# Where the softmax denominators of a streaming encoder layer are added up: diagonal exponentials on GpSimd and VectorE, one ones-product a step

## The chip, the cores and the metric

The kernel runs on one core of a Trainium2 chip. Its time is the device time of one execution in microseconds; the time of a kernel is the median of its runs. The engines that matter are TensorE (PE, with its weight loads listed apart as PEld), VectorE (DVE), ScalarE (ACT), GpSimd (POOL) and the queues that issue DMAs (SP's above all).

## What is computed

One layer of a hybrid encoder, in one step for 2048 new frames of a prompt and for 8 streams of 16 frames each that have 1024 cached frames. The part that the change touches is the attention of both groups, with 8 heads of 64 columns:

```python
def _attend(q, k, v, cum_q, cum_k, q_pos, k_pos):
    s = jnp.einsum('bqhd,bkhd->bhqk', q, k, preferred_element_type=jnp.float32) * (HEAD_DIM ** -0.5)
    s = s + (cum_q[..., :, None] - cum_k[..., None, :])
    mask = k_pos[None, :] <= q_pos[:, None]
    s = jnp.where(mask, s, NEG_INF)
    p = jax.nn.softmax(s, axis=-1)
    return jnp.einsum('bhqk,bkhd->bqhd', p.astype(v.dtype), v)
```

Before it lie the conditioning, a normalisation and the input projection, beside it a convolution branch with a normalisation over channels, and behind it the output projection and a gated feed-forward network. All of it is in 32-bit floats.

## The kernel before

The kernel goes through the stages in order: input projections, queries and keys, attention (627 to 1187 us of the span), output projection, feed-forward network.

**Steps of the attention.** The prompt's attention is 16 steps: four pairs of heads `p` by four blocks of 512 queries `qb`. A step goes over `4 * qb + 4` tiles of 128 keys (`kt`). For each tile and each of the two heads `h`, TensorE makes the scores `s` with keys on the partitions and queries on the columns (lines 1035 and 1041, with a mask product on line 1043 where the tile lies on the diagonal), and ScalarE makes the exponentials `e` (line 1045). The last four tiles of a step are the diagonal ones; their columns begin at `off` = 0, 128, 256 and 384, so they are 512, 384, 256 and 128 wide. Two tiles later `values` adds the product of `e` with V into the bank `pv` (line 999).

**Denominators.** The sum of the exponentials over the keys is a sum over partitions, done with a product by a matrix of ones 32 columns wide into the bank `sm` (`add_up`, line 988). Each of the four groups of 32 PE columns holds a term. For tiles before the diagonal the exponentials are first added up elementwise into two tiles `sums`: those of head 0 by GpSimd (line 1011), those of head 1 by VectorE (line 1012, shown under the helper's line 1105). Diagonal tiles went to TensorE one by one: at the second diagonal tile four products of 512 columns (the two `sums` and the first diagonal tile; in the steps with `qb` = 0, which have no tile before the diagonal, the first two diagonal tiles), and at the fourth the rest. `end_of_step` copies `sm`, sends its rows to memory, brings them back turned, inverts them on VectorE and multiplies `zc` by the inverse; the last step does it with a product by `four` on TensorE instead, into a bank of the group `cv`.

**Maxima.** The exponentials need the largest score of each query. A second pass of score products (`mx`, line 952, with a mask product on line 956 at the diagonal) runs ahead of the scores, and VectorE reduces each to its maximum (`M`, line 957). There are 320 of them, two PSUM banks (`cv`), and they run up to `LEAD` = 48 tiles ahead in the order of emission.

**Order.** A scheduler orders each engine's instructions by priority, with extra order edges written by hand (`after`). Three matter here. A score product may not stand before the `last_product` emitted ahead of it, so ones-products hold the scores back (line 1038). A score product stands behind a maximum's product 32 to 42 tiles ahead. And every VectorE operation issued through `late(..., self.last_max)` stands behind the last maximum emitted by then. Each engine works through its list in order.

**Background.** Into the steps are woven the channel normalisation of the convolution branch (`conv_norm`, tiles `cy`, `cm`, `cr`, `cq`; its GpSimd operations stand behind the last addition of exponentials) and the attention of the eight streams (`sample_scores`, `sample_values`; tiles `S`, `ST`, `En`, `rsx`, `lane`). A stream's denominators were eight products with one column: for each of four pairs of heads one of `rsx` (sums over cached keys) with `fold`, and one of `EnT` (the new frames) with ones.

## Time and profile before

| | us |
|---|---|
| median of 3 runs | 2798.58 |
| the three runs | 2797.13, 2798.58, 2804.48 |
| profiled execution | 2804.35 |
| its span | 2802.6 |
| attention in the span | 627 to 1187 |

The profiled execution was 5.77 us above the median. Columns of the rows below: a group's row gives line, engine, operation, output and inputs, then count, busy microseconds and the mean of one in nanoseconds, then the idle time before them and what ended it. A row in order of time gives start and length in microseconds. A 32-bit product of TensorE shows as two records, a score product as one.

### The profile page before, as it was taken

What the parts mean: (1) busy time and instruction counts of PE and PEld (TensorE: products, weight loads), DVE (VectorE), ACT (ScalarE), POOL (GpSimd) and SP (SyncE); (2) the same over time, 40 slices, a digit from 0 to 9 for tenths busy, and PEclk for the clock granted to TensorE, in tenths of its full rate; (3) what the DMA queues carried; (4) which work ended last, traced back from release to release, by engine and by line L of the source; (5) the groups of instructions that cost most, each with busy time, mean ns of one, the idle gap of its engine ahead of it and who ended that gap; (6) DMA issues with size and microseconds to landing.
All of it is one profiled execution on the core that took longest, in us unless ns stands there. A gap on an engine that the chain in (4) does not pass through costs nothing. (4 is left out here: it accounts for less than half of the span.)

```text
span 2802.6 us, 49271 instructions
## 1 busy us (share of the span) xinstructions
PE 2734.4 (98%) x17042; PEld 2407.4 (86%) x17042; DVE 2023.4 (72%) x4116; ACT 1235.4 (44%) x2472; POOL 499.6 (18%) x678
## 2 busy tenths in 40 slices
PE   7999999999999999999999999999999999999999
PEld 6999988864445555499999999999999999999999
DVE  2798898964656666545397989877887778676765
ACT  4543323343444333444354446444554446555552
POOL 3555411323443121214201121000000000000000
PEclk9999999989999999999999999999999999999999
DMA  9753568673536576165576869866786769787873
GB/s 330 252 186 115 186 213 269 200 201 87 149 94 199 163 238 211 53 219 185 168 262 209 300 198 313 282 213 214 248 279 213 224 194 319 243 288 254 277 250 116
DMA packets 416978, 603.57 MB, mean 215 GB/s; under 512 B 65140, under 2 KB 280340, under 8 KB 414680
## 3 DMA queue, kind: packets, MB, share of 16 engines
q1 hardware_dynamic: 416520, 600.05, 67.1%
q8 instruction: 134, 2.20, 0.3%
q14 instruction: 116, 0.95, 0.1%
q0 software_dynamic: 208, 0.37, 0.0%
HBM read 426.00 MB, written 174.25 MB: 214 GB/s over the span
## 5 line engine op out<-in xcount | busy, mean ns | idle before, releaser
L1663 PE MATMUL z<-rT,rW 128*128 128x360 f32 (+1 forms) x8316 | 1382.8, 328 | 4.6 <-ACT eU L1682 1.2
L1663 PEld LDWEIGHTS z<-rT,rW 128*128 128x128 f32 x8316 | 1378.6, 188 | 6.8 <-DVE e L1685 1.8
L1367 ACT ACTIVATE rW<-rR 128x512 fp32r<-128x512 f32 x714 | 434.8, 617 | 391.1 <-PE z L1663 274.4
L1368 DVE TENSOR_TENSOR rW<-rR,rW 128x512 fp32r<-128x512 f32 x714 | 477.8, 674 | 162.6 <-ACT rW L1367 159.1
L712 DVE SCALAR_TENSOR_TENSOR cv<-cu,cpar,cv 128x384 f32<-128x384 f32 x580 | 311.6, 614 | 2.3 <-ACT cv L710 2.2
L957 DVE TENSOR_REDUCE M<-mx 128x1 f32<-128x512 f32 (+2 forms) x320 | 190.6, 605 | 167.8 <-PE mx L952 125.0
L1045 ACT ACTIVATE e<-s 128x512 f32<-128x512 f32 (+3 forms) x320 | 166.4, 531 | 291.6 <-PE s L1041 165.0
L524 PE MATMUL z<-hqx,wqh 128*128 128x384 f32 (+1 forms) x768 | 197.6, 333 | 1.4 <-DVE logf L359 1.4
L1367 ACT ACTIVATE rT<-traw 128x360 fp32r<-128x360 f32 (+1 forms) x315 | 149.6, 501 | 86.8 <-DMA traw<-gt_d 53.8
L1368 DVE TENSOR_TENSOR rT<-traw,rT 128x360 fp32r<-128x360 f32 (+1 forms) x315 | 157.9, 531 | 38.0 <-ACT rT L1367 37.5
L999 PE MATMUL pv<-e,V 128*64 128x512 f32 (+3 forms) x640 | 158.7, 569 | 0.0
L952 PE MATMUL mx<-K,Q 96*128 96x512 f32 (+2 forms) x320 | 142.8, 460 | 11.8 <-DVE M L957 10.7
L952 PEld LDWEIGHTS mx<-K,Q 96*128 96x128 f32 x320 | 62.6, 198 | 103.7 <-DVE M L957 48.1
L524 PEld LDWEIGHTS z<-hqx,wqh 128*128 128x128 f32 x768 | 136.1, 188 | 17.8 <-issue 12.4
L1351 PE MATMUL acc<-ch,woh 128*128 128x360 f32 (+1 forms) x384 | 128.2, 336 | 8.5 <-ACT ch L1367 3.4
L1035 PE MATMUL s<-Q,K 128*128 128x512 f32 (+3 forms) x320 | 131.5, 411 | 0.0
L1351 PE MATMUL acc<-ch,wol 128*128 128x360 f32 (+1 forms) x384 | 128.1, 334 | 0.0
L524 PE MATMUL z<-hqx,wql 128*128 128x384 f32 (+1 forms) x384 | 126.6, 330 | 0.0
L1591 DVE TENSOR_TENSOR rR<-rR 128x512 f32<-128x512 f32 (+1 forms) x136 | 93.2, 703 | 44.7 <-DMA rR<-w_down 41.8
L1351 PE MATMUL acc<-cl,woh 128*128 128x360 f32 (+1 forms) x384 | 123.9, 333 | 0.0
L1041 PE MATMUL s<-Q,K 128*128 128x512 f32 (+3 forms) x320 | 120.2, 375 | 0.0
L1011 POOL TENSOR_TENSOR sums<-e,sums 128x512 f32<-128x512 f32 x72 | 93.9, 1304 | 115.9 <-ACT e L1045 114.9
(316 smaller groups left out, 3746.8 us busy)
## 6 DMA issues: line engine op xcount, KB each, us to landing
rR<-sup_d SPq DMA_DIRECT2D x176, 256.0 KB
rR<-w_gate SPq DMA_DIRECT2D x132, 256.0 KB
traw<-gt_d SPq DMA_DIRECT2D x154, 180.0 KB
rR<-w_down SPq DMA_DIRECT2D x104, 256.0 KB
rR<-sdn_d SPq DMA_DIRECT2D x96, 256.0 KB
rR<-w_up SPq DMA_DIRECT2D x88, 256.0 KB
sup_d<-rR SPq DMA_DIRECT2D x88, 256.0 KB
wa<-w_ada SPq DMA_DIRECT2D x16, 1024.0 KB
```

The lines of the kernel that those rows point to most:

```text
L524: nc.tensor.matmul(z[:, :n], w[:, m], x[:, :n], start=(c == 0 and k == 0), stop=(c == CB - 1 and k == 2))
L712: self.pin(nc.vector.scalar_tensor_tensor(dst, src, w, acc[i], ALU.mult, ALU.add))
L952: self.mx.append(nc.tensor.matmul(mx[:, :w], Q2[0:AUX, h, j * P:(j + 1) * P], K2[kb][0:AUX, h, :w], start=True, stop=not diag))
L957: self.last_max = nc.vector.tensor_reduce(M[:, i, kb:kb + 1], mx[:, :w], AX.X, ALU.max)
L999: product = nc.tensor.matmul(z[0][HD * h:HD * h + HD, off:], V[kt // 4][:, kt % 4, HD * h:HD * h + HD], es[h][:, off:], start=(kt == 0), s ...
L1035: first = nc.tensor.matmul(s[:, off:], K1[kb][:, h, sl], Q1[:, h, off:], start=True, stop=False)
L1041: self.last_s = nc.tensor.matmul(s[:, off:], K2[kb][:, h, sl], Q2[:, h, off:], start=False, stop=not diag)
L1045: self.last_piece = nc.scalar.activation(e[:, off:], s[:, off:], AF.Exp)
L1351: self.nc.tensor.matmul(z[:, :n], w[:, m], y, start=(first and i == 0 and k == 0), stop=(last and i == len(terms) - 1 and k == 2))
L1367: copy = self.nc.scalar.activation(hi, raw, AF.Copy)
L1368: engine.tensor_tensor(lo, raw, f32(hi), ALU.subtract)
L1663: nc.tensor.matmul(z, W[:, x, m], t[:, y, :w], start=(k == 0 and i == 0), stop=(k == n - 1 and i == 2))
```

## The change

1. Exponentials of all tiles, the diagonal ones too, are added into the two `sums` tiles, by GpSimd for head 0 and VectorE for head 1 (`settle`). It is called before the second score of the tile after, and not two tiles later with the values. In the steps with `qb` = 0 the first 128 columns are copied first.
2. A step makes its two ones-products once, over 512 columns, after its last value product.
3. `sm` has 64 rows and two parts instead of four, so fewer DMAs, and VectorE's addition of the two parts goes.
4. The last step's spread goes into the bank `ss` (the lane's) instead of one of `cv`.
5. A stream's denominators: VectorE adds the new frames' sums to `rsx`, GpSimd multiplies them into `parts` (128x128), and TensorE makes one product with ones.
6. `conv_norm` yields once more before its second mean.

```diff
-        def add_up(terms, last=False):
-            if not started:
-                z.append(self.bank("tr", "sm"))
+        def add_up(out, terms):
             behind = self.last_product
-            for i, (g, o, x) in enumerate(terms):
-                self.last_product = nc.tensor.matmul(z[1][32 * g:32 * g + 32, o:], self.ones[:, 0:32], x[:, o:], start=(g not in started),
-                                                     stop=last and g not in [t[0] for t in terms[i + 1:]], tile_position=(0, 32 * g))
+            for h, x in enumerate(terms):
+                self.last_product = nc.tensor.matmul(out[32 * h:32 * h + 32], self.ones[:, 0:32], x, start=True, stop=True, tile_position=(0, 32 * h))
                 self.after(self.last_product, behind)
+
+        def settle(kt, off, es):
+            dve = lambda op, *args: self.late(op, self.last_max)(*args)
+            if kt == 0:
+                held.extend(es)
+                return
+            x, y = held
+            if kt == 1:
+                acc.extend(wk.tile([P, 512], F32, tag="acc", name="sums", bufs=4) for h in range(2))
+                if off:
+                    nc.gpsimd.tensor_copy(acc[0][:, :off], x[:, :off])
+                    dve(nc.vector.tensor_copy, acc[1][:, :off], y[:, :off])
+            else:
+                x, y = acc
+            self.last_add = nc.gpsimd.tensor_tensor(acc[0][:, off:], es[0][:, off:], x[:, off:], ALU.add)
+            dve(nc.vector.tensor_tensor, acc[1][:, off:], es[1][:, off:], y[:, off:], ALU.add)
...
-            if d == 3:
+            if kt == nkt - 1:
                 zc = wk.tile([P, 512], F32, tag="zc", name="zc")
                 self.last_exp = nc.scalar.copy(zc, z[0])
-                add_up(held, True)
-                self.end_of_step(p, qb, zc, z[1])
-            elif d == 1:
-                n = 4 if qb else 2
-                add_up(held[:n])
-                del held[:n]
+                sums = self.bank("tr", "sm")
+                add_up(sums, acc)
+                self.end_of_step(p, qb, zc, sums)
...
             for h in range(2):
+                if h and self.unsettled:
+                    self.unsettled.pop(0)()
...
                 if h:
+                    self.unsettled.append(partial(settle, kt, off, es))
                     self.waiting.append((values, kt, off, es))
...
-            spread = self.bank("cv", "R")
-            nc.tensor.matmul(spread, self.four, sm, start=True, stop=True)
+            spread = self.bank("ss", "R")
+            nc.tensor.matmul(spread, self.two, sm, start=True, stop=True)
...
-            if qb:
-                self.after(nc.vector.tensor_tensor(w[:, 0], w[:, 0], w[:, 1], ALU.add), self.last_max)
-            self.after(nc.vector.reciprocal(w[:, 0], w[:, 0]), self.last_max)
+            self.after(nc.vector.reciprocal(w, w), self.last_max)
...
+        rn = sm.tile([32, NP], F32, tag="rn", name="rn")
+        parts = sm.tile([P, NP, 32], F32, tag="parts", name="parts")
+        self.dve("tensor_reduce", rn, self.En[:, :, :QS], AX.X, ALU.add)
+        self.dve("tensor_tensor", rs[:32], rs[:32], rn, ALU.add)
+        self.gp(parts, self.fold.unsqueeze(1).broadcast_to([P, NP, 32]), rs.unsqueeze(2).broadcast_to([P, NP, 32]), ALU.mult)
...
-        for g in range(NP):
-            r = slice(32 * g, 32 * g + 32)
-            self.pe(den[r], self.fold, rs[:, g:g + 1], start=True, stop=False, tile_position=(0, 32 * g))
-            self.pe(den[r], EnT[:QS, g], self.ones[:QS, 0:1], start=False, stop=True, tile_position=(0, 32 * g))
+        self.pe(den, parts.rearrange("p g r -> p (g r)"), self.ones[:, 0:1], start=True, stop=True)
```

What this does to the order is seen at three places. The first is TensorE's list at the end of the third step (`p` = 0, `qb` = 2). Before, from the first ones-product (the numbers behind names are buffers; `masks` products belong to the maximum ahead of them):

```order
L988 MATMUL sm_7897<-sums_7610,ones_115 32x512 [waits Pool_49]
L952 MATMUL mx_7804<-K25_6650,Q21_6636 128x128 [waits DVE_49]
L956 MATMUL mx_7804<-masks_4135 128x128
L952 MATMUL mx_7818<-K24_6647,Q21_6636 128x512 [waits DVE_49]
L952 MATMUL mx_7831<-K25_6650,Q21_6636 128x256 [waits DVE_49]
L956 MATMUL mx_7831<-masks_4135 128x128
L968 MATMUL pz_7835<-ident_99,Z_0_6621 128x128 [waits DVE_49]
L988 MATMUL sm_7897<-sums_7611,ones_115 32x512 [waits DVE_49]
L988 MATMUL sm_7897<-e_7777,ones_115 32x512
L988 MATMUL sm_7897<-e_7798,ones_115 32x512
```

The same place after the change:

```order
L988 MATMUL sm_7952<-sums_7578,ones_115 32x512 [waits Pool_49]
L954 MATMUL mx_7881<-K24_6647,Q21_6636 128x512 [waits DVE_49]
L954 MATMUL mx_7904<-K25_6650,Q21_6636 128x512 [waits DVE_49]
L958 MATMUL mx_7904<-masks_4135 128x128
L954 MATMUL mx_7913<-K24_6647,Q21_6636 128x512 [waits DVE_49]
L954 MATMUL mx_7925<-K25_6650,Q21_6636 128x128 [waits DVE_49]
L958 MATMUL mx_7925<-masks_4135 128x128
L954 MATMUL mx_7940<-K24_6647,Q21_6636 128x512 [waits DVE_49]
L988 MATMUL sm_7952<-sums_7579,ones_115 32x512 [waits DVE_49]
L1034 MATMUL s_7965<-Q1_7644,K10_6633 128x512 [waits Activation_49]
```

Between the ones-product of GpSimd's sums and that of VectorE's stood three maxima products, and now five. Before, ten of the sixteen steps had two to nine maxima there, 35 in all (the four steps with `qb` = 0 had no such place, and the last two steps none left); now fourteen steps have them, 80 in all: thirteen in the first step, seven in the second, five in each of the twelve after. The last two steps have none, and their two ones-products stand side by side.

The second place is VectorE's list there, after the change:

```order
L959 TENSOR_REDUCE M_1_6656<-mx_7881 128x1
L1103 TENSOR_TENSOR sums_7579<-e_7865,sums_7579 128x256
L1095 TENSOR_TENSOR zc_7551<-zc_7551,aR_7558 128x512
L959 TENSOR_REDUCE M_1_6656<-mx_7904 128x1
L959 TENSOR_REDUCE M_1_6656<-mx_7913 128x1
L1103 TENSOR_TENSOR sums_7579<-e_7898,sums_7579 128x128
L959 TENSOR_REDUCE M_1_6656<-mx_7925 128x1
L959 TENSOR_REDUCE M_1_6656<-mx_7940 128x1
```

The last addition (128 columns, buffer `e_7898`), for which the second ones-product waits, moved behind the third of the five maxima; the last diagonal tiles had no addition on VectorE before.

The third place is GpSimd's list at the end of the eighth step (`p` = 1, `qb` = 3), where the last chunk of `conv_norm` ends. Before:

```order
L1105 TENSOR_TENSOR cy<-cy,cmu 128x128 x4
L1011 TENSOR_TENSOR sums<-e,sums 128x512 x4
L1105 TENSOR_TENSOR cy<-cy,cr 128x128 x4
L1153 MEMSET En 32x128
L1156 MEMSET Qbd 128x1024
```

After:

```order
L1103 TENSOR_TENSOR cy<-cy,cmu 128x128 x4
L1005 TENSOR_TENSOR sums<-e,sums 128x512 x5
L1005 TENSOR_TENSOR sums<-e,sums 128x384
L1005 TENSOR_TENSOR sums<-e,sums 128x256
L1103 TENSOR_TENSOR cy<-cy,cr 128x128 x4
L1005 TENSOR_TENSOR sums<-e,sums 128x128
```

The step's last addition, which the first ones-product waits for, now stands behind the four operations on `cr`; before, no ones-product had to wait for anything behind them in this step.

## The prediction

> **What bounds the kernel now.** The page comes first: TensorE is busy nearly all the time, so only what TensorE does or waits for can move the end. Then the table by windows, for the attention alone (columns after the length: busy microseconds and count of PE, PEld, DVE, ACT, POOL, then the granted TensorE clock, the DMA share and GB/s).

> ```profile
> PE 2734.4 (98%) x17042; PEld 2407.4 (86%) x17042; DVE 2023.4 (72%) x4116; ACT 1235.4 (44%) x2472; POOL 499.6 (18%) x678
> 627.00:1187.00 560.00, 547.29 (x3607) 283.68 (x3606) 326.54 (x678) 227.74 (x513) 165.88 (x164) 0.98 0.51 150
> ```

> Of 560 us TensorE shows 12.7 idle; VectorE is 58% busy, GpSimd 30%. The view of waits says who waits for whom in the same stretch:

> ```profile
> ACT e L1045 <- PE s L1041: 165.0, 115, 11.4
> PEld mx L952 <- DVE M L957: 40.0, 59, 3.1
> ```

> ScalarE's exponentials wait for TensorE, not the reverse. The one engine that TensorE often waits for is VectorE, in the maxima pass with its two banks. So the attention is bound by TensorE, with VectorE close behind where maxima stand thick.

> **Part 1, the ones-products.** The first row counts the records of line 988 in the attention. I price each product by its slot, the time from its start to the start of what follows it, in the list of TensorE's instructions in order of time:

> ```profile
> 627.00:1187.00 560.00, 51.48 (x304) 11.86 (x304) 0.98 0.51 150
> ...
> 1046.70 1.05 PE L988 MATMUL sm<-sums,ones 128*32 128x512 f32 x2
> 1047.68 0.33 PE L1105 MATMUL lane<-ident,ob 128*128 128x128 f32 x1
> ...
> 1050.80 0.62 PE L988 MATMUL sm<-e,ones 128*32 128x512 f32 x2
> ...
> 1051.78 0.50 PE L1035 MATMUL s<-Q,K 128*128 128x512 f32 x1
> ...
> 1056.11 1.27 PE L988 MATMUL sm<-e,ones 128*32 128x384 f32 x12
> 1057.31 0.39 PE L1035 MATMUL s<-Q,K 128*128 128x256 f32 x1
> 637.40 1.49 PE L988 MATMUL sm<-e,ones 128*32 128x384 f32 x12
> 638.82 0.50 PE L952 MATMUL mx<-K,Q 96*128 96x512 f32 x1
> ```

> A single product of 512 columns has a slot of 0.98 us; three side by side in other column groups (1050.80) have 0.98 too. The six smaller ones have 1.20, or 1.42 where `qb` = 0. Before, then: twelve steps of 0.98 + 0.98 + 1.20 = 3.16, which is 37.9, and four of 0.98 + 1.42 = 2.40, which is 9.6; 47.5 in all. After, by the order shown above, fourteen steps issue their two products apart (1.96) and two issue them together (0.98): 29.4. **Gain 18.1 us**, on the path, since nothing covers TensorE.

> **Part 2, the wait between the two.** The scores of the next tiles are held until the second product is issued, and TensorE has only maxima (and lane work) to do until VectorE's last addition is through. The trace has this place already, shorter:

> ```profile
> 887.62 0.73 PE L952 MATMUL mx<-K,Q 96*128 96x512 f32 x2
> 888.90 0.44 PE L952 MATMUL mx<-K,Q 96*128 96x384 f32 x1 [0.56 <-DVE M L957]
> ...
> 889.63 0.62 PE L988 MATMUL sm<-e,ones 128*32 128x512 f32 x2
> 886.02 0.42 DVE L957 TENSOR_REDUCE M<-mx 128x1 f32<-128x256 f32 x1
> 888.16 0.69 DVE L957 TENSOR_REDUCE M<-mx 128x1 f32<-128x512 f32 x1 [1.72 <-PE mx L952]
> 888.88 0.69 DVE L1105 TENSOR_TENSOR sums<-e,sums 128x512 f32<-128x512 f32 x1
> L957 DVE TENSOR_REDUCE M<-mx 128x1 f32<-128x512 f32 (+2 forms) x283 | 170.0, 608 | 162.5 <-PE mx L952 122.1 <-PE mx L956 39.1
> ```

> It lasts from 887.62 to 889.63, 2.01 us: 0.54 until the first maximum starts on VectorE, one maximum, one addition. TensorE's own work in it is three maxima at about 0.37 (0.73 for the first two), 1.1, so 0.9 is lost. After, three maxima and the additions of 256 and 128 columns stand before the second product: 0.54 + 3 x 0.69 + 0.42 + 0.24 = 3.27. The two additions have no row; I take the 0.42 of a maximum 256 wide, and 0.24 as an estimate for half of that. TensorE's work is 5 x 0.37 = 1.85, so 1.42 is lost, 0.52 more than before. Nine steps of 0.52 are 4.7. Three steps with `qb` = 0, which had no such place, lose 1.42 each, 4.3. The first step gets thirteen maxima, eleven before its last addition: 0.54 + 11 x 0.69 + 1.4 for four operations is 9.5, less 4.8 of work, so 4.7. The second step had nine maxima and now has seven:

> ```profile
> 655.90 0.73 PE L952 MATMUL mx<-K,Q 96*128 96x512 f32 x2
> ...
> 662.79 1.06 PE L988 MATMUL sm<-sums,ones 128*32 128x512 f32 x1
> ```

> From 6.9 less 3.3 of work to about 5.2 less 2.6: a gain of 1.0. **Loss 12.7 us.** Bounds: nothing, if the rounds behind a burst, which then have fewer maxima, run as much faster; and 45 more maxima at 0.608, 27 us, if none of their TensorE work is saved elsewhere. I keep 12.7, the count from the rows.

> **Part 3, more additions.** A step had `4 * qb - 1` additions on each engine where `qb` is above 0, and now has `4 * qb + 3`: 144 instead of 84, and four copies.

> ```profile
> L1105 DVE TENSOR_TENSOR sums<-e,sums 128x512 f32<-128x512 f32 x72 | 58.3, 809 | 1.8 <-ACT e L1045 1.3
> L1011 POOL TENSOR_TENSOR sums<-e,sums 128x512 f32<-128x512 f32 x72 | 93.9, 1304 | 115.9 <-ACT e L1045 114.9
> ```

> On GpSimd they cost at most 60 x 1.3 = 78 us, to 244 of 560, hidden as long as its list isn't blocked (first rival). On VectorE some 30 have their price in part 2. The other 32 stand among maxima in ordinary rounds and delay a bank's return. Bounds: nothing, or 0.81 each, 26 us. I take TensorE's idle time of before over the additions of before, 12.7 / 84 = 0.15: **loss 4.8 us**.

> **Part 4, a stream's denominators.**

> ```profile
> 1038.69 0.22 PE L1105 MATMUL lane<-rsx,fold 128*32 128x1 f32 x2
> ...
> 1039.89 0.64 PE L1105 MATMUL lane<-kc,Qbd 128*32 128x128 f32 x14
> L288 PE MATMUL pm<-sum,ma 128*128 128x9 f32 x64 | 7.6, 247 | 0.0
> ```

> Eight products take 1.20 us, 9.6 for eight streams. One full-array product takes 7.6 / 32 = 0.24 alone, and at most the 0.98 of a ones-product with its change of tiling; I take 0.4: 3.2. **Gain 6.4** (1.8 to 7.7). The chain to it gets a reduction, an addition and a product on GpSimd:

> ```profile
> 1046.59 0.20 DVE L1105 TENSOR_REDUCE mx<-S 32x4 f32<-32x64 f32 x1
> ```

> They run beside the transposes and the 36 value products of the stream, which TensorE needs first; uncovered they would be some 0.2 + 0.2 + 0.7 (half an addition) each, 9 us; I take nothing.

> **Part 5, the end, and the rest.**

> ```profile
> 1190.46 0.33 PE L1351 MATMUL acc<-ch,wol 128*128 128x368 f32 x1
> 1191.91 0.68 PE L1351 MATMUL acc<-ch,woh 128*128 128x368 f32 x1 [1.12 <-DVE aR L1075]
> 1188.50 3.36 DVE L1075 RECIPROCAL aR<-R 128x512 f32<-128x512 f32 x1 [11.54 <-PE R L1074]
> ```

> The output projection's fourth bank waits 1.12 us for the last reciprocal, which reads its spread there. With the spread in the bank used last, six products' time more goes by: **gain 1.1** (0 to 1.3). Fewer DMAs on SP's queue, the missing addition of parts and the added yield lie beside TensorE's work; without that cover a lane would come a round later, and no tail follows, since the lane ends before the last step in both orders. I take nothing.

> **Sum.** -18.1 + 12.7 + 4.8 - 6.4 - 1.1 = -8.1. Against the profiled execution's own 2804.35 (a span of 2802.6 with 1.75 around it) that gives 2796.2; that execution was 5.8 above the median of the runs shown, so on the median the forecast is 2798.6 - 8.1 = 2790.5.

> **Rivals.**

> *GpSimd comes late.* The first ones-product needs GpSimd's last addition. GpSimd works in order, and the lanes make it wait:

> ```profile
> 759.13 1.60 POOL L1105 TENSOR_TENSOR cy<-cy,cr 128x256 f32<-128x256 f32 x2 [12.31 <-DVE cr L1105]
> ```

> In two places of the new order (the one shown, and the start of the fifth step) such operations stand ahead of the last additions of a step. If a wait like this 12.3 falls there, two rounds of some 3 us hide half, and 6 us come through at each: -8.1 + 12 = +4, 2802.5. For it: the row. Against it: the scheduler placed the other additions where VectorE's `cr` is long done. Chance 0.15.

> *The bursts cost nothing.* If maxima pulled into a burst spare their TensorE time and VectorE's waits later, parts 2 and 3 vanish: -18.1 - 6.4 - 1.1 = -25.6, 2773. For it: TensorE's waits for maxima come from rounds that would be lighter. Against it: TensorE idles in the burst, and that time cannot be saved. Chance 0.20 for -15 to -26.

> *Slower: the granted clock falls in the bursts.* In the longest burst of before it did, from about 3.4 us after its start:

> ```profile
> 656.00:660.00 4.00, 2.53 (x7) 1.15 (x7) 3.56 (x6) 0.00 (x0) 0.00 (x0) 0.93 0.70 197
> 660.00:664.00 4.00, 3.60 (x11) 1.27 (x10) 3.56 (x8) 0.00 (x0) 0.00 (x0) 0.50 0.04 1
> 664.00:668.00 4.00, 4.00 (x21) 1.86 (x21) 0.00 (x0) 1.36 (x3) 0.00 (x0) 0.72 0.24 50
> 886.00:890.00 4.00, 3.23 (x13) 0.93 (x14) 2.23 (x5) 0.23 (x1) 0.00 (x0) 1.00 1.02 372
> ```

> That cost 4 x (0.07 + 0.50 + 0.28) = 3.4 us. A burst of 2 us (886) kept full clock. The new ones are 3.3 us, with a slot of 0.98 at each end. If each of thirteen lost half as much, 1.7, that is 22 us: +14, 2812.6; five of them already eat the gain. Chance 0.20. [...]

> **Chances.** The forecast has 0.45, with its own range of -2 to -15, half of it beyond 0.3%. A measurement of this kernel can tell about 0.3%, 8.4 us, from no change. Faster by more: half the forecast and the second rival, 0.43. Within: the other half and most of the first, 0.35. Slower: the third and a little of the first, 0.22. The range runs from 2774, short of the second rival's end, to 2812, where the third is nearly whole.

> **What would show it.** TensorE's ones-products should fall from 304 records to 64, with slots of 0.98 where they stand apart. The stretch between the two of a step should be 3 to 3.6 us in the twelve later steps and about 9 in the first, with VectorE's addition 128 wide as what ends it. The product with `parts` should have a slot under 0.5 and no wait for GpSimd. No wait for `aR` should be left at the output projection. I am wrong if TensorE waits for GpSimd ahead of a first product, if the clock column shows 0.5 behind most bursts, or if ordinary rounds with a narrow addition get longer by more than 0.15.

## The result, and the profile after

The kernel after takes 2824.12 us (median of 5 runs, 2814.61 to 2827.61); before takes 2798.58. The ratio is 1.008, with a 95% interval of 1.0056 to 1.0103. The forecast was 2790.5, with a range up to 2812: the sign is wrong, and the time lies outside the range.

The profiled execution took 2827.61 us. From the attention's start at 627 to the last spread (1210.8, before 1187.3) it is 583.8 us against 560.3, 23.5 more; behind it nothing differs by a microsecond. First the page and the table by windows of the kernel after, with the columns of the prediction's rows:

```profile
PE 2729.9 (97%) x16690; PEld 2397.8 (85%) x16690; DVE 2065.4 (73%) x4185; ACT 1235.2 (44%) x2472; POOL 557.0 (20%) x748
627.00:1210.80 583.80, 544.00 (x3264) 275.11 (x3263) 363.31 (x749) 229.87 (x519) 232.47 (x236) 0.95 0.48 144
```

TensorE has 343 records fewer in the attention, and is busy 3.3 us less; but it is idle 39.8 us instead of 13.0, and the granted clock is 0.95 instead of 0.98. The groups of TensorE and the view of waits, in the attention:

```profile
L954 PE MATMUL mx<-K,Q 96*128 96x512 f32 (+3 forms) x284 | 126.1, 462 | 29.0 <-DVE M L959 25.5 <-DMA Q<-q_d 2.3 <-DVE mrow L972 0.4
L988 PE MATMUL sm<-sums,ones 128*32 128x512 f32 x64 | 37.9, 711 | 0.0
L1103 PE MATMUL lane<-ones,parts 128*128 128x1 f32 x16 | 3.0, 257 | 0.0
PEld mx L954 <- DVE M L959: 60.1, 87, 2.7
PE mx L954 <- DVE M L959: 25.5, 43, 2.4
```

The ones-products fell from 304 records to 64, as foretold. The idle time stands before maxima, which wait for VectorE to empty a bank: 25.5 us of it. Here is one of those places, between the two ones-products of a step; TensorE's list in order of time, then VectorE's:

```profile
865.22 1.04 PE L988 MATMUL sm<-sums,ones 128*32 128x512 f32 x2
866.20 0.76 PE L954 MATMUL mx<-K,Q 96*128 96x512 f32 x2
866.80 0.22 PE L958 MATMUL mx<-masks 128*128 128x128 f32 x1
868.41 0.50 PE L954 MATMUL mx<-K,Q 96*128 96x512 f32 x1 [1.38 <-DVE M L959]
870.28 0.47 PE L954 MATMUL mx<-K,Q 96*128 96x128 f32 x1 [1.37 <-DVE M L959]
...
872.09 1.92 PE L988 MATMUL sm<-sums,ones 128*32 128x512 f32 x2
```

```profile
864.48 1.46 DVE L1103 TENSOR_TENSOR sums<-e,sums 128x384 f32<-128x384 f32 x1
...
866.33 0.74 DVE L1103 SCALAR_TENSOR_TENSOR cm<-cr 128x256 f32<-128x256 f32 x2
867.00 0.75 DVE L1103 TENSOR_TENSOR cm<-cm,cvar 128x256 f32<-128x256 f32 x2
867.67 0.68 DVE L959 TENSOR_REDUCE M<-mx 128x1 f32<-128x512 f32 x1
868.27 0.41 DVE L1103 TENSOR_TENSOR sums<-e,sums 128x256 f32<-128x256 f32 x1
868.61 0.68 DVE L1095 TENSOR_TENSOR zc<-zc,aR 128x512 f32<-128x512 f32 x1
869.21 0.41 DVE L1103 SCALAR_TENSOR_TENSOR cr<-cm,cr 128x256 f32<-128x256 f32 x1
...
871.23 0.28 DVE L1103 TENSOR_TENSOR sums<-e,sums 128x128 f32<-128x128 f32 x1
```

VectorE is never idle from 864.48 to 871.5; between the maxima stand operations of the channel normalisation (`cm`, `cr`), the multiplication of `zc`, and an addition that takes 1.46 us (GpSimd's own addition runs from 864.24 to 865.52 beside it; 384 columns took 0.55 where GpSimd was still). The second ones-product can't go before the addition at 871.23. The stretch from first to second product is 6.87 us here; over the twelve later steps it is 6.1 in the mean (4.2 to 8.6), and 11.35 and 5.65 in the first two. The second product then takes 1.92 instead of 1.04. The windows of this place tell why (the last three columns are the granted clock, the DMA share and GB/s):

```profile
862.17:865.59 3.42, 3.06 (x16) 1.70 (x15) 2.77 (x5) 2.37 (x7) 1.28 (x1) 1.00 0.02 4
865.59:869.00 3.41, 1.94 (x6) 0.67 (x4) 3.41 (x9) 0.45 (x1) 0.00 (x0) 1.00 0.03 1
869.00:872.41 3.41, 1.74 (x4) 0.97 (x5) 2.92 (x8) 0.00 (x0) 2.71 (x4) 0.50 0.21 77
872.41:875.83 3.42, 3.42 (x6) 1.16 (x4) 0.47 (x1) 1.18 (x2) 3.09 (x5) 0.50 0.00 1
875.83:879.24 3.41, 3.41 (x16) 1.50 (x15) 1.36 (x3) 1.75 (x3) 2.07 (x2) 1.00 0.92 297
```

The windows are chosen so that the clock changes at their edges. In the second TensorE is busy 1.94 of 3.41 us, still at full clock; the third is at half clock, and little busy too; the fourth, full of work, is at half clock as well, and the fifth at full clock again. A half window I count as 1.71 us of TensorE's work lost, half of its 3.41, an estimate from its clock of 0.50. The attention after has 18 of them, and 15 stand in or behind nine of the fourteen places between two ones-products; before has 8.

So I split an attention's time in three: what TensorE is **idle**, what it loses in **half windows** (1.71 each), and the rest, its **work** at full clock. From before to after that is +26.8, +17.1 and -20.4, together the 23.5.

### The profile page after: what moved, and what is told of

It is laid out like the page before. It is cut to its first block, busy times and chain, and to the rows that moved or that the text cites. A ratio compares the mean times of both kernels' runs of the same rounds, so it can differ in the third digit from the quotient of the medians.

```text
span 2825.8 us, 48838 instructions
## 1 busy us (share of the span) xinstructions
PE 2729.9 (97%) x16690; PEld 2397.8 (85%) x16690; DVE 2065.4 (73%) x4185; ACT 1235.2 (44%) x2472; POOL 557.0 (20%) x748
## 5 line engine op out<-in xcount | busy, mean ns | idle before, releaser
L1005 POOL TENSOR_TENSOR sums<-e,sums 128x512 f32<-128x512 f32 (+3 forms) x128 | 145.7, 1138 | 259.3 <-ACT e L1044 258.5
L1034 PE MATMUL s<-Q,K 128*128 128x512 f32 (+3 forms) x320 | 135.7, 424 | 3.9 <-ACT e L1044 3.9
L1351 PE MATMUL acc<-ch,woh 128*128 128x360 f32 (+1 forms) x384 | 127.2, 334 | 7.7 <-ACT ch L1367 4.0
L1034 PEld LDWEIGHTS s<-Q,K 128*128 128x128 f32 x320 | 63.4, 198 | 83.8 <-issue 43.1
L1351 PE MATMUL acc<-ch,wol 128*128 128x360 f32 (+1 forms) x384 | 127.3, 331 | 0.0
L1351 PE MATMUL acc<-cl,woh 128*128 128x360 f32 (+1 forms) x384 | 123.6, 332 | 0.7 <-DVE cl L1368 0.7
```

The costliest lines, as they stand in the source:

```text
L1005: self.last_add = nc.gpsimd.tensor_tensor(acc[0][:, off:], es[0][:, off:], x[:, off:], ALU.add)
L1034: first = nc.tensor.matmul(s[:, off:], K1[kb][:, h, sl], Q1[:, h, off:], start=True, stop=False)
L1351: self.nc.tensor.matmul(z[:, :n], w[:, m], y, start=(first and i == 0 and k == 0), stop=(last and i == len(terms) - 1 and k == 2))
```

## The experiments

Beside the four groups of runs the kernel before took 2801.32, 2800.53, 2800.45 and 2801.23 us; the runs' ratios are to these. The parts of the attention come from one profiled execution each, up to 6.1 us from its kernel's median, so differences of a few us in them can be those of one execution.

| kernel | median us | ratio to before (95%) | attention | idle | half windows | work |
|---|---|---|---|---|---|---|
| before | 2798.58 | | 560.3 | 13.0 | 8 | 533.7 |
| after | 2824.12 | 1.0056 to 1.0103 | 583.8 | 39.8 | 18 | 513.3 |
| e1_pin | 2762.79 | 0.9851 to 0.9878 | 521.8 | 30.4 | 8 | 477.8 |
| e2_fill | 2822.39 | 1.0060 to 1.0086 | 578.2 | 12.6 | 7 | 553.7 |
| e3_rest | 2785.32 | 0.9933 to 0.9960 | 544.1 | 14.8 | 3 | 524.2 |
| e4_before_pin | 2790.10 | 0.9942 to 0.9974 | 549.9 | 16.6 | 10 | 515.2 |
| e5_free | 2782.89 | 0.9914 to 0.9949 | 539.6 | 28.1 | 9 | 496.1 |
| e6_lead44 | 2789.84 | 0.9947 to 0.9978 | 549.8 | 32.1 | 11 | 498.9 |
| e7_best | 2772.52 | 0.9870 to 0.9921 | 533.6 | 40.8 | 10 | 475.7 |
| e8_double | 2770.37 | 0.9875 to 0.9913 | 529.5 | 33.0 | 6 | 486.2 |
| e9_old_den | 2760.24 | 0.9839 to 0.9871 | 521.5 | 25.7 | 6 | 485.6 |
| e10_gp_divide | 2762.20 | 0.9849 to 0.9880 | 520.2 | 27.1 | 8 | 479.4 |
| e11_gp_inv10 | 2768.34 | 0.9874 to 0.9914 | 522.7 | 34.1 | 8 | 475.0 |
| e12_no_den | 2801.68 | 0.9988 to 1.0008 | 562.0 | 15.3 | 9 | 531.4 |

**The order edge (e1_pin).** In after, VectorE's additions stand behind the last maximum emitted, which is up to 16 ahead of what the scores need. This run puts them behind the maximum that the scores of that tile need:

```diff
...
                     self.last_max = nc.vector.tensor_reduce(M[:, i, kb:kb + 1], mx[:, :w], AX.X, ALU.max)
+                    self.reduced.append(self.last_max)
...
-            dve = lambda op, *args: self.late(op, self.last_max)(*args)
+            at = min(self.nscore + AHEAD + min(self.nscore // 5, 10), len(self.mx)) - 1
+            dve = lambda op, *args: self.late(op, self.reduced[at])(*args)
```

> The kernel after, with one edge changed: VectorE's additions of exponentials stand behind the maximum that the scores of that tile need, not behind the last maximum emitted (up to 16 ahead). In TensorE's order the two ones-products of a step then stand side by side in 15 of 16 steps, with no maximum between. Theory W (the wait between the two ones-products is what made the change slower): TensorE's idle time in the attention falls from 39.1 us to under 13, the clock there goes from 0.95 to 0.98, and the time is that of before less some 14 x 0.98 more of slots and less the terms for ones-products and denominators, about 2760, at most 2785. Theory C (the 60 more additions slow VectorE and GpSimd down wherever they stand): still 2810 to 2824, since no addition is taken away.

It takes 2762.79: 61 us less than after, and 1.35% (1.2 to 1.5) less than before. Nothing else in the kernel differs, and no addition was taken away, so the place of the additions in VectorE's list is what made the change slower. The attention in the table by windows, and TensorE's list at the end of a step now (the profile of this run):

```profile
627.00:1148.80 521.80, 491.43 (x3250) 263.15 (x3246) 367.71 (x746) 227.73 (x514) 236.69 (x235) 0.97 0.53 161
...
903.50 1.05 PE L989 MATMUL sm<-sums,ones 128*32 128x512 f32 x4
904.48 0.50 PE L954 MATMUL mx<-K,Q 96*128 96x512 f32 x1
904.82 0.40 PE L1036 MATMUL s<-Q,K 128*128 128x512 f32 x1
```

Both products of the step (four records) take one slot of 0.98, and scores follow at once. Of the 62 us of the attention, 35.5 are work, 17.1 half windows, 9.4 idle time. Counted product by product at full clock in the two traces, the slots of the ones-products make about 12 of the work, those of the maxima with their masks 10, and those of scores and values 9. A maximum's product with a wait behind it took its whole 0.50 (868.41 above), where in a run of products its slot was 0.30 (866.20: 0.60 for two). Why scores and values have shorter slots too is not shown.

The idle time did not fall under 13, as expected, but to 30. It now has few long pieces. One of them, on TensorE and on VectorE:

```profile
912.99 0.79 PE L954 MATMUL mx<-K,Q 96*128 96x512 f32 x1 [4.95 <-DVE M L959]
```

```profile
911.91 0.69 DVE L1097 TENSOR_TENSOR zc<-zc,aR 128x512 f32<-128x512 f32 x1 [5.54 <-DMA aR<-inv_d]
912.52 1.01 DVE L959 TENSOR_REDUCE M<-mx 128x1 f32<-128x256 f32 x2
```

VectorE waits for the inverse on its way back, with maxima queued behind it. The faster kernel reaches this place earlier than the DMA does.

**Something to do in the wait (e2_fill).** Five ones-products of 256 columns more in each step, each behind one of the last five maxima:

```diff
+                if h:
+                    for m in self.mx[-5:]:
+                        again = nc.tensor.matmul(out[0:32, 0:256], self.ones[:, 0:32], terms[0][:, 0:256], start=True, stop=True, tile_position=(0, 0))
+                        self.after(again, m)
+                        self.after(again, behind)
...
-                self.after(self.last_product, behind)
+                self.after(self.last_product, again if h else behind)
```

> The kernel after, with five more ones-products of 256 columns in each step, each behind one of the last five maxima emitted, which write again what the first ones-product wrote: TensorE has something to do while it waits for VectorE. Theory K (most of the loss is the granted clock that falls to half behind the bursts, since TensorE idles in them): the half-clock stretches go, the clock of the attention rises from 0.95 towards 0.98, and the time falls by 5 to 15 us in spite of 75 more products. Theory W without the clock (only the wait itself counts): the time stays within 5 us of 2824 or rises by what the 75 products take, up to 75 x 0.4 = 30 us.

```profile
627.00:1205.20 578.20, 565.60 (x3401) 279.16 (x3399) 362.11 (x743) 226.27 (x512) 231.12 (x232) 0.98 0.48 144
```

The clock did what theory K says (0.95 to 0.98), but the time stayed where theory W has it: the median is 2822.39, as after within the spread, and not 5 to 15 us less. 40 us of work were added, more than the 30 reckoned with; idle time fell by 27.2 and half windows from 18 to 7, 18.8 us. So the half windows come from the lulls: with TensorE fed, and VectorE no faster, most of them go. Four of the seven left are in the first step, where the fillers stand behind five maxima of thirteen.

**Scores set free (e5_free).** The two ones-products stay where they were, but no longer count as `last_product`, behind which scores must stand.

```diff
-                self.last_product = nc.tensor.matmul(out[32 * h:32 * h + 32], self.ones[:, 0:32], x, start=True, stop=True, tile_position=(0, 32 * h))
-                self.after(self.last_product, behind)
+                product = nc.tensor.matmul(out[32 * h:32 * h + 32], self.ones[:, 0:32], x, start=True, stop=True, tile_position=(0, 32 * h))
+                self.after(product, behind)
```

> The kernel after, with VectorE's additions where they were, but the scores no longer held behind the ones-products (only behind the value products, as before): 5 maxima still stand between the two ones-products of a step, and now 4 to 10 score products with their values too. Theory H (the maxima alone between the two cost nothing; it is the held scores that leave TensorE without work): near the first run, 2762 to 2780, TensorE idle under 25 us, few half-clock stretches. Theory V (VectorE's late addition costs by itself, through the banks of the sums or the order of the maxima): it stays above 2800.

2782.89, 41 us less than after: nearest to theory H and far from theory V, though 3 us above theory H's range, with 28.1 us of idle time where under 25 was expected, and nine half windows. So VectorE's late addition costs most where the scores are held behind it. It has 18 us more of work than e1_pin; 11 of them are ones-products, which keep a slot each.

**A shorter lead (e6_lead44).** `LEAD = 44` in place of 48.

> The kernel after with LEAD 44 in place of 48, so that the last maximum emitted is less far ahead: 1 maximum instead of 5 between the two ones-products in eight steps, and 9 and 6 in the first two (13 and 7 before); in the later steps of the third and fourth pair the second product moves a round or more behind the scores. Theory W: most of the 62 us between after and the first run come back, 2765 to 2785. If the length of the burst doesn't matter but only that the products stand apart (14 slots of 0.98, 13.7 us), 2805 to 2812.

2789.84: above the upper end of theory W, and far below the other. Half windows fall from 18 to 11 and work by 14 us, but idle time only to 32. Fewer maxima in the lull help, by a second road; a shorter lead also made single waits elsewhere, up to 5.3 us.

**The same edge in before (e4_before_pin).**

> The kernel before with the same changed edge as the first run: its ten steps with 2 to 9 maxima between the first and the later ones-products lose them. Theory W: the gain is the idle time there, 0.9 us in nine steps and 3.6 in the second, with some half-clock time, 8 to 15 us, so 2784 to 2791; a good deal less than what the same edge gives the kernel after. Rival (additions placed earlier help VectorE in general, and not the wait): as much as in the first run, 30 us or more.

2790.10, 11 us less than before, within theory W's range. But its parts are not those of theory W: idle time is 3.6 us more and half windows two more, and work is 18.5 less, of which some 10 are ones-products that share slots now. So the old edge cost before something too, in slots more than in waits, and it is worth five times as much where the change had put 80 maxima. With the new edge in both kernels the rest of the change is worth some 27 us (2790.10 to 2762.79); with the old one it cost 25.5.

**The other edits alone (e3_rest, e12_no_den).** Before, with a stream's denominators by one product, the spread in `ss`, one more yield and one buffer for the inverses; then the same without the denominators.

> The kernel before, with only the other edits: a stream's denominators by one product, the last spread in the lane's bank, one more yield (and one buffer instead of two for the inverses, so that it fits). By the prediction's terms: 6.4 + 1.1 less, about 2791. Rival: the chain through VectorE and GpSimd to the product with parts is not covered, 9 us more, about 2807. If these edits were the cause of the slower time, 2815 or more.

> The kernel of the third run (2785) without its change of the streams' denominators: before with the last spread in the lane's bank, one more yield in the channel normalisation, one buffer for the inverses. If the 16 us of the third run came from the denominators (their slots fell by some 9 us, and fewer half-clock stretches followed), this one is at 2797 to 2801. If they came from where the extra yield and the spread put the other work, 2785 to 2790, and the ninth run, in which the denominators were worth nothing, speaks for this one.

2785.32 and 2801.68: the denominators alone are worth 16 us here, and the rest nothing. Of that 7.2 is work, as the slots say (9.7 us before, 2.3 after). The others are half windows, 9 without the edit and 3 with it, 10.2 us. The profile of before shows a half window behind eight products of one column:

```profile
1034.89:1038.30 3.41, 3.41 (x74) 2.32 (x70) 1.61 (x3) 0.00 (x0) 0.00 (x0) 1.00 1.04 282
1038.30:1041.72 3.42, 3.42 (x42) 2.41 (x42) 2.22 (x5) 0.00 (x0) 0.00 (x0) 1.00 0.35 74
1041.72:1045.13 3.41, 3.41 (x13) 1.59 (x11) 0.80 (x4) 0.77 (x2) 0.00 (x0) 0.50 0.94 229
```

The second window holds those products (1038.69 to 1039.89). TensorE is shown busy in all of it, and yet the third is at half clock. Five of before's seven half-clock stretches begin at the end of a window with these products.

**The denominators in the pinned kernel (e9_old_den).** e1_pin with the eight products of before.

> The kernel of the first run with a stream's denominators made by the eight products of before. By the prediction's fourth term 6.4 us more than the first run (2763), so about 2769; by the slots of the profiles (9.7 us of such products before, 2.4 after, and 1.3 more on the value products ahead of them) 7 to 9 more, 2770 to 2772. If the edit is worth what the third run gained over before, 14 us or more, 2777.

A miss: 2760.24, no slower than e1_pin. The work is 7.8 us more, as the slots say, but idle time is 4.7 less and two half windows are missing. The same edit is worth 16 us in one kernel and nothing in the other. That what TensorE saves here is waited away elsewhere fits the parts, but wasn't tried by itself.

**More additions (e7_best, e8_double).** For e8_double the kernel of e7_best (below) got one more VectorE operation behind each of its 60 additions of a diagonal tile:

```diff
+            if kt >= 4 * qb:
+                dve(nc.vector.tensor_tensor, acc[1][:, off:], es[1][:, off:], acc[1][:, off:], ALU.max)
```

> The kernel of the run before this one, with each of VectorE's 60 additions of a diagonal tile followed by one more operation of the same size, which changes no value (the larger of the sum and the addend). It measures what such an operation costs in the round where it stands. Prediction's price: 0.15 each, 9 us more than that run. Nothing, if VectorE has the room: within 3 us. The bound where each delays a bank's return by its whole duration, 60 x 0.5 = 30 us or more.

2770.37 against 2772.52: no price to be seen, though the runs of each kernel spread over 10 us and more and would hide one of a few us. Its parts differ (10.5 us more work, 7.8 less idle, four half windows fewer), but the sum is what counts here. At these places VectorE has room for 60 more such operations.

**Later and elsewhere (e7_best, e10_gp_divide, e11_gp_inv10).** Three tries at the waits that e1_pin left: all steps of a division later; the multiplication on GpSimd; and that with the inverse two scores later.

```diff
-((3, load), (8, invert), (13, back), (20, divide))
+((3, load), (12, invert), (17, back), (28, divide))
```

```diff
-            self.after(nc.vector.tensor_tensor(zc, zc, R, ALU.mult), self.last_max)
+            self.gp(zc, zc, R, ALU.mult)
```

> The kernel of the first run, with the denominators' way back asked for later: the inverse 12 scores after the step instead of 8, the load of it 17 instead of 13, the multiplication 28 instead of 20. In the first run VectorE waited 5.5, 5.9 and 4.5 us for those DMAs with maxima queued behind, and TensorE 4.95, 6.66 and 2.79 for the maxima, each with half clock behind it (some 12 us of the 13.6 lost there). Theory: these waits go, 12 to 25 us less than 2763, so 2738 to 2752. Rival: the waits only move to other transfers or to ScalarE's exponentials, 2758 to 2766.

> The kernel of the first run with the last step of a division (the product of zc with the inverse) on GpSimd instead of VectorE, at the same place. The maxima then don't queue behind the wait for the inverse's DMA, which cost TensorE 4.95 us once and some half clock behind it. Theory: 5 to 10 us less than 2763, 2753 to 2758. Rival: GpSimd now waits ahead of its additions, and the first ones-product for them, 2765 or more.

> The kernel of the run before this one, with the inverse asked for 10 scores after a step instead of 8. VectorE's waits of 5.9 and 4.5 us for the sums' way back, with maxima behind, get shorter by two scores' time (about 3 us). Theory: another 5 to 10 us less, 2745 to 2752. Rival, from the seventh run: the order on the DMA queue shifts and a later load waits instead, as much or more than the run before this one.

The three theories missed: 2772.52, 2762.20 and 2768.34. In e7_best and e11_gp_inv10 the rival's mechanism came, a wait that moves to another transfer, in e7_best at more than its price. In e10_gp_divide GpSimd waits 42 us for the inverse instead, without harm, but VectorE still waits 15.6 for the sums on their way back. VectorE's waits for the sums and for the inverse, 21.6 us in e1_pin, fell to 5.8 in e7_best, and in e11_gp_inv10 none of them is left; but in both TensorE got a longer one. In e7_best, on TensorE and on the DMA queue of SP:

```profile
979.27 0.64 PE L1105 MATMUL lane<-kc,Qbd 128*32 128x128 f32 x16 [0.94 <-DVE S L1105]
992.55 1.22 PE L954 MATMUL mx<-K,Q 96*128 96x512 f32 x2 [12.64 <-DMA Q<-q_d]
```

```profile
979.11 1.21 SPq L915 DMA_DIRECT2D K<-k_d  x1
980.36 1.10 SPq L947 DMA_DIRECT2D Q<-q_d  x1
```

The queries for the next maxima were issued only at 980.36, behind the streams' loads, and TensorE waited until 992.55. In all six kernels with the edge of e1_pin in after TensorE has one wait of 5.9 to 12.6 us that ends between 981 and 994. In e7_best, e8_double and e11_gp_inv10 (11.0 to 12.6) it is for these queries. In e1_pin, e9_old_den and e10_gp_divide (5.9 to 7.7) it is for `mrow`, which on VectorE stands behind a wait of 5.2 to 6.9 us for the sums on their way back. In all six the load that is waited for was issued on this queue behind the streams' loads. That these are the common cause is my reading, and not shown. The best kernels are e9_old_den, e10_gp_divide and e1_pin (2760.24 to 2762.79), which can't be told apart.

## Why the prediction was wrong

**Part 1, the ones-products: right at full clock.** A slot was 0.98 where the clock was full, as foretold. But seven second products stood in half windows and took about 1.84, so all slots are 34.8 us instead of 29.4, and the gain is 12 instead of 18.1. Counted at full clock the slots are 27.9 against 46.1 before, a gain of 18.2; the other 6 belong to the clock.

**Part 2, the wait between the two: this is the step that failed.** It put the stretch at 3.27 us behind a slot of 0.98, 4.25 in all, and the loss at 12.7. It measured 6.1 in the mean of the twelve, and TensorE's idle time rose by 26.8. The sum counted VectorE's maxima and two additions alone; in most places its list also holds `zc`, the channel normalisation or a stream's scores, which stand among the same maxima. Where it holds but one narrow reduction more, in the fourth step, the stretch is 4.23, as foretold, and the clock stays full:

```profile
770.51 1.04 PE L988 MATMUL sm<-sums,ones 128*32 128x512 f32 x2
...
774.74 1.04 PE L988 MATMUL sm<-sums,ones 128*32 128x512 f32 x2
```

The first two steps were sized about right (11.35 and 5.65 against 10.5 and 6.2). A smaller part is the additions themselves: 256 and 128 columns took 0.41 and 0.28 in the mean where GpSimd was still (priced at 0.42 and 0.24), and 0.68 and 0.41 beside its instructions.

**The clock: priced at nothing in the sum.** It cost 17.1 us. The third rival had the mechanism and the price (1.7 us at each of thirteen, 22 us; one half window is 1.71), and was given a fifth of the chance; against it stood a stretch of 2 us in before that kept its clock. It named this as a sign of being wrong, and nine of the fourteen places show it. The clock went with the length: the two shortest stretches (4.23 and 4.63 us) kept it, and nine of the other twelve (5.53 to 11.35) lost it. A window of 3.41 us that falls into the lull nearly whole would fit this; that is my reading, and not shown. If so, the same wrong length hid both losses. TensorE was not without work ahead of the drop: in the place shown above the window ahead of the half clock had 1.94 of 3.41 us busy.

**Part 3, more additions: 4.8 foretold, nothing to be seen** (e8_double), in a kernel without the bursts; a price of this size is within the spread there.

**Part 4, a stream's denominators: 6.4 foretold; the slots gave 7.2** (9.6 to 2.4). In the time they were worth 16 us in before, 10.2 of it half windows, and nothing in e1_pin. In one place of e1_pin the product waits for GpSimd's `parts` (2.5 us); in after never.

**Part 5, the end: the wait right, the gain not to be seen.** No wait for `aR` is left; one of 0.65 for `cl` came. From the spread's start to the end of the first eight products of `cl` it was 9.07 us, and is 7.43; but before had a half window there (from 1191.9), which alone is worth 1.7, and from the spread to the end of the span both take 1615 us.

```profile
1210.80 1.12 PE L1074 MATMUL R<-sm,two 64*128 64x512 f32 x2 [0.70 <-ACT sm L1069]
1216.62 1.61 PE L1351 MATMUL acc<-cl,woh 128*128 128x368 f32 x8 [0.65 <-DVE cl L1368]
```

**The first rival** (GpSimd late) did not come: no ones-product waits for GpSimd. **The second** (bursts cost nothing, 25.6 below before) is near what the change gives with the new edge in both kernels, 27 us.

In the sum: work -20.4 against -24.5 foretold (ones-products and denominators gave 25, and the slots of the maxima took some 5 back), waits +26.8 against +17.5, clock +17.1 against 0. These three make 30.5 of the 31.4 us between the foretold -8.1 and the +23.3 of the profiled executions.

## What to carry to other kernels

An order edge on "the last one emitted" moves with the emission's lead: when work is put behind it that the other engine needs soon, count what is pulled ahead of it, on both engines, everything in their lists and not only the kind that the change is about. In this kernel two engines that waited for each other, in lulls of 4.23 to 11.35 us, paid twice, 26.8 us more in waits and 17.1 in the clock afterwards; look at the clock in windows right behind each lull. And a gain that frees a bound engine may only be worth what the next thing in line lets through: the denominators gave 16 us in before and nothing in e1_pin, where TensorE is left with waits of 4.95 and 6.66 us.

## What the runs showed of the hardware

Of the windows at full clock, all 38 in which TensorE was busy for 1.60 us or less were followed by one at half clock. Of the 65 from there to 2.44 us 19 were. Above that only 14 of 2006 were, 12 of them shown as fully busy, in kernels with the eight products of one column. So the busy time that the profile shows does not settle it alone. In e9_old_den the same products brought no half window; what decides there stays open.

In before VectorE's additions were slower beside GpSimd's instructions: those of 512 columns took 0.64 to 0.71 us where GpSimd ran during less than three tenths of them (64), and 1.21 in the mean and up to 1.73 where it ran for more (20).
